# RWKV projections by way of DRAM, one eviction per scan half step and a pinned TensorE order in a hybrid decoder layer

## The chip, the cores and the metric

The kernel runs on one core of one Trainium2 chip. The metric is the device time of one execution in microseconds (us), and of several runs the median. Engines are named as the profile names them: PE (TensorE matmul), PEld (TensorE weight load, overlapping PE), DVE (VectorE), ACT (ScalarE), POOL (GpSimd), SP (SyncE, which issues most DMAs).

## What is computed

One decoder layer in fp32 for 512 prompt tokens and 8 decode tokens (520 columns, kept as two halves of 260), model width 2048:

```python
mod = silu(c) @ w_ada + b_ada                      # 6 x 2048: shift, scale, gate, twice
h = modulate(rmsnorm(x), sh1, sc1)
q, k, v, p_rwkv = split(h @ w_in)                  # 1024 + 2 x 256 attention, 3360 RWKV columns
att = banded_attention(q, k, v)                    # window 128, ALiBi, sinks
# RWKV-7, 16 heads of 64: per token, with decay w, a = -kk, b = kk * iclr
S = S * w + (S a) b^T + v k^T ;  y = S r           # then group norm, bonus, gate
x = x + gt1 * (concat(att, rw) @ w_out)
x = x + gt2 * (swiglu(modulate(rmsnorm(x), sh2, sc2)))
y = rmsnorm(x)
```

New key and value rows, the RWKV states and the last projection rows are outputs too.

## The kernel before, in words

**Main products.** All large products are built from `mm3` (L94): a weight tile is split into a high part `wh` (ACT cast, L88) and a low part `wl` (DVE, L91), and three fp32r products (`wh` by the high and low part of the activations, `wl` by the high part), each for two halves of 260 columns, make six main products per 128 rows of contraction. `main_tile` (L103) does one 128-column tile of `w_in`: 16 times six products into a PSUM tile `pm`, with a 256 KB weight load (`raw`, SP) per 24 products. After every six it calls `pump`.

**Background jobs.** Everything else in the RWKV phase consists of Python generators on the list `bg`. `pump` (L123) is a turn: it moves a model clock on and lets each job whose modelled time has come issue its next piece, up to the next `yield`. The model clock is kept by `Paced` (L30): each operation that a job issues through `self.px` adds an estimated duration to its engine's clock. That fixes the program order; the tile scheduler then reorders the instructions of each engine by a model of its own, so that the order of TensorE is the scheduler's. Line L49, in `Paced`, is the line that the profile shows for everything issued through it.

**The jobs.** `ada_gen` (L304) computes the four later parts of `mod`: for each of 16 x 16 steps a 256 KB load `ar` (a ring of three buffers in the pool `w`) and four products with 32 columns side by side (`ada`, L314), and two yields. For each of the eight head pairs `hp`: `rwkv_prep1` (L547) makes decay, key and removal factors from the key columns; `rwkv_prep2` (L641) does receptance, value and bonus; `rwkv_rest` (L690) solves a triangular system per chunk of 32 tokens on DVE (`Tt`, 31 steps, its input `As` by way of DRAM), runs the scan, and then group norm and gate.

**The scan.** For each of 16 chunks (L742 on) there are two half steps, each in a turn of its own. First, for each of the two heads `e`, a product of `L3` with the state `Z[:, c, e]` into 32 rows of the PSUM tile `psc`, at array columns 96 and 64; DVE evicts head 0 and ACT head 1 into `Z`. Second, for each head a product with `LS` into 64 rows, at array columns 0 and 64; DVE and ACT evict them, multiplied by the chunk decay `PC`, as the next chunk's state. The profile's names are `psc<-Z,L` for the first half step and `psc<-Z,LS` for the second (a digit at a name's end is left out, so `L3` reads `L`).

**Where the projections wait.** The RWKV tiles of `w_in` (8 + hp key, hp receptance, 16 + hp value) are evicted by ACT straight into one of four SBUF buffers `pc` (`w_in_tile`, L440). The main stream therefore waits for a free buffer; while it would wait it takes `filler` tiles (L452): the 12 attention tiles, which ACT copies to a buffer `sp` of the `ar` ring and SP stores to DRAM (L463).

Of the kernel before, what the change touches and what calls it, by code (L numbers as in the profile page):

```python
# [28 lines left out]
I_WA, I_G0, I_G1 = 24, 25, 26  # L29

# [21 lines left out]

class PacedCore:
# [10 lines left out]
class Kern:  # L64
    def __init__(self, tc, I, O, upto="all"):
        self.tc, self.nc, self.I, self.O, self.upto = tc, tc.nc, I, O, upto
# [67 lines left out]
    def start(self, gen):  # L134
        self.bg.append([gen, 0.0])
# [13 lines left out]
    def run(self):  # L149
        tc, nc, I = self.tc, self.nc, self.I  # L150
        R = dict(side="right")
        with ExitStack() as st:
# [3 lines left out]
            self.load_consts()  # L156
            self.catd = [self.dr.tile([P, 512], F32, name=f"catd{i}") for i in range(16)]
# [10 lines left out]
            with ExitStack() as st2:  # L168
# [28 lines left out]
                self.drain()  # L197
                right.close()
# [105 lines left out]
    def ada_gen(self):  # L304
        nc = self.px
        for c in (GT1, SH2, SC2, GT2):
            for q in range(4):
                ci = c // 4 + q
                ps = self.hold("ada")
                for k in range(KD):  # L310
# [8 lines left out]
                    yield  # L319
                    yield  # L320
# [49 lines left out]
    def startup(self):  # L370
# [25 lines left out]
        self.pcs, self.ring, self.used = {}, [], set()  # L396
# [5 lines left out]
        self.start(self.seq(self.h_parts(xk, rstd), self.ada_gen()))  # L402
# [72 lines left out]
    def rwkv_phase(self):  # L475
# [36 lines left out]
        nc.scalar.copy(self.SG1[64:128], self.SG1[0:64].bitcast(F32))  # L512
        pairs = [{"ready": True, "done": True, "chain": True, "prep1": True, "solved": True}] * 3
        for hp in range(8):
            d = {"hp": hp, "prev": pairs[-1], "prev2": pairs[-2], "prev3": pairs[-3]}
            pairs.append(d)
            for idx, job in ((8 + hp, self.seq(self.rwkv_prep1(d), self.rwkv_rest(d))), (hp, None),
                             (16 + hp, self.rwkv_prep2(d))):
                if idx not in self.pcs:
                    self.w_in_tile(idx)  # L520
                if job:
                    self.start(job)
# [14 lines left out]
    def recip(self, t, n=4):  # L537
        w = 512 // n
        for i in range(n):
            self.px.vector.reciprocal(t[:, i * w:(i + 1) * w], t[:, i * w:(i + 1) * w])  # L540
            yield

# [4 lines left out]
    def rwkv_prep1(self, d):  # L547
        nc, I, rp, rc = self.px, self.I, self.rp, self.rc
        hp = d["hp"]
        while not {"ready", "prep1"} <= d["prev"].keys() or "done" not in d["prev3"]:  # L550
            yield
# [7 lines left out]
        d["PC"] = PC = rc.tile([P, 16], F32, tag="PC", bufs=3, name=self.nm("PC"))  # L559
# [4 lines left out]
        for _ in range(3):  # L564
            yield
# [7 lines left out]
        nc.scalar.activation(A, pw, AF.Tanh, bias=self.w0h[:, hp:hp + 1], scale=0.5)  # L573
        ta = t512("tD")
# [19 lines left out]
        yield from self.recip(nrm)  # L594
# [8 lines left out]
        yield  # L603
# [4 lines left out]
        nc.vector.tensor_copy(PC, c3(B)[:, :, 31])  # L608
        d.update(kf=kf, B=B, KB=KB, t512=t512)
        yield  # L610
# [7 lines left out]
        while "solved" not in d["prev"]:  # L618
            yield
# [15 lines left out]
        q2[0].dma_start(self.ABd[hp].rearrange("(q c) t s -> (c t) q s", c=4), AB)  # L635
        for g in range(4):
            q2[g % 2].dma_start(self.As[32 * g:32 * g + 32].rearrange("p (t s) -> p t s", s=32), self.ABd[hp])
        d["prep1"] = True
        yield

    def rwkv_prep2(self, d):  # L641
        nc, I, rp, rc = self.px, self.I, self.rp, self.rc
        while "kf" not in d or "done" not in d["prev2"]:
            yield
# [1096 lines left out]
```

## Time and profile before

| | |
|---|---|
| median of 3 runs | 2659.92 us (2652.76 to 2669.23) |
| profiled execution | 2657.76 us, span 2656.0 us, mean granted TensorE clock 0.985 |
| start and first norm | 0 to 137 us |
| RWKV phase, from the first `ada` product to the first output projection | 137 to 927 us |
| attention and output projection | 927 to 1209 us |
| FFN in | 1209 to 2130 us |
| FFN out | 2130 to 2656 us |

The page gives busy times per engine; the windows give them by stage. A matmul's end is modelled and matmuls overlap, so a PE busy share near one says little: what the spacing of products is, is read from the starts in the timeline. In the groups, "idle" is an engine's idle time just before such instructions, with what ended it. A row of a tile's view gives shortest, median and longest duration in ns.

### The profile page before, as it was taken

The numbers are of one execution on the slowest core, as the hardware profiler recorded it, in microseconds if no ns is written. First come the engines' busy times: TensorE is split into PE (matmuls) and PEld (weight loads), VectorE is DVE, ScalarE is ACT, GpSimd is POOL, SyncE is SP. The second block draws the span as 40 slices with busy tenths as digits, with TensorE's granted clock in tenths as the row PEclk, the third lists the DMA queues.
The fourth block names the chain that finished last, engine by engine and source line by source line (L and its number), as shares of the span: only waits on it lengthen the run. The fifth ranks groups of instructions, "written<-read, shape, count | busy, mean of one in ns | idle before, by whom it ended". The sixth has DMA issues, their size and how long they took to land. (4 is left out here: it accounts for less than half of the span.)

```text
span 2656.0 us, 59166 instructions
## 1 busy us (share of the span) xinstructions
PE 2554.5 (96%) x23373; PEld 2340.7 (88%) x23373; DVE 1723.8 (65%) x3880; ACT 1105.9 (42%) x2153; POOL 382.5 (14%) x525
## 2 busy tenths in 40 slices
PE   7899999999999999998999999999999999999997
PEld 4677777888787889898999999999999999999997
DVE  5466767777657444678777777777777763444456
ACT  3133444545533324547544444444444532222225
POOL 0012112112112000021111212111121100000004
PEclk9999999999989999999999999999999999999999
DMA  9855445455546675245777777777777552333333
GB/s 347 294 165 154 152 126 162 149 166 160 159 153 207 203 251 146 94 160 183 191 201 204 193 208 198 191 207 198 194 208 200 155 184 92 124 125 102 116 105 106
DMA packets 241704, 460.22 MB, mean 173 GB/s; under 512 B 32353, under 2 KB 44561, under 8 KB 241393
## 3 DMA queue, kind: packets, MB, share of 16 engines
q1 hardware_dynamic: 206880, 379.88, 44.5%
q0 software_dynamic: 33904, 75.50, 13.4%
q8 instruction: 183, 3.00, 0.5%
q10 hardware_dynamic: 640, 1.05, 0.2%
q14 instruction: 97, 0.79, 0.1%
HBM read 421.73 MB, written 35.59 MB: 172 GB/s over the span
## 5 line engine op out<-in xcount | busy, mean ns | idle before, releaser
L88 ACT CAST wh<-raw 128x512 fp32r<-128x512 f32 (+2 forms) x410 | 246.9, 606 | 510.5 <-PE pf L98 278.9
L98 PE MATMUL pf<-go,wh 128*128 128x260 f32 x2560 | 414.1, 281 | 0.0
L91 DVE TENSOR_TENSOR wl<-raw,wh 128x512 fp32r<-128x512 f32 (+2 forms) x410 | 283.8, 694 | 200.4 <-ACT wh L88 194.8
L98 PEld LDWEIGHTS pf<-go,wh 128*128 128x128 f32 x2560 | 354.0, 188 | 0.1
L98 PE MATMUL pm<-hH,wh 128*128 128x260 f32 (+1 forms) x1248 | 301.3, 319 | 7.3 <-ACT wh L88 6.7
L1269 ACT CAST wh<-sr 128x512 fp32r<-128x512 f32 x320 | 198.1, 621 | 261.7 <-PE pm L1439 232.0
L1270 DVE TENSOR_TENSOR wl<-sr,wh 128x512 fp32r<-128x512 f32 x320 | 220.6, 690 | 83.0 <-ACT wh L1269 75.9
L98 PE MATMUL pm<-hH,wl 128*128 128x260 f32 (+1 forms) x1248 | 265.4, 292 | 5.2 <-DVE wl L91 5.1
L98 PE MATMUL pf<-go,wl 128*128 128x260 f32 x1280 | 267.7, 282 | 0.0
L1439 PE MATMUL pm<-xT,wh 128*128 128x260 f32 x1408 | 263.2, 286 | 4.4 <-DVE pc L1516 4.3
L98 PE MATMUL pm<-hL,wh 128*128 128x260 f32 (+1 forms) x1248 | 263.4, 291 | 0.0
L1439 PE MATMUL pm<-T,wh 128*128 128x260 f32 x1408 | 257.6, 283 | 0.0
L98 PEld LDWEIGHTS pm<-hH,wh 128*128 128x128 f32 (+1 forms) x1248 | 196.5, 191 | 57.8 <-issue 31.6
L1439 PEld LDWEIGHTS pm<-xT,wh 128*128 128x128 f32 x1408 | 216.9, 188 | 11.0 <-DVE pc L1516 6.1
L1439 PEld LDWEIGHTS pm<-T,wh 128*128 128x128 f32 x1408 | 216.9, 188 | 0.0
L98 PEld LDWEIGHTS pm<-hH,wl 128*128 128x128 f32 (+1 forms) x1248 | 197.4, 192 | 16.0 <-DVE wl L91 8.7
L1439 PE MATMUL pm<-B0H,wl 128*128 128x260 f32 x704 | 201.4, 286 | 9.6 <-DVE wl L1270 9.1
L98 PEld LDWEIGHTS pm<-hL,wh 128*128 128x128 f32 (+1 forms) x1248 | 196.9, 191 | 7.5 <-issue 5.2
L1439 PE MATMUL pm<-B0H,wh 128*128 128x260 f32 x704 | 200.3, 285 | 2.0 <-DVE acct L1206 1.7
L98 PEld LDWEIGHTS pf<-go,wl 128*128 128x128 f32 x1280 | 200.9, 188 | 0.0
L1439 PE MATMUL pm<-B0L,wh 128*128 128x260 f32 x704 | 198.9, 282 | 0.0
L1439 PE MATMUL pm<-T,wl 128*128 128x260 f32 x704 | 198.7, 282 | 0.0
(427 smaller groups left out, 5243.8 us busy)
## 6 DMA issues: line engine op xcount, KB each, us to landing
ar<-in_w_ada SPq DMA_DIRECT2D x256, 256.0 KB, 3.1
sr<-in_w_fi SPq DMA_DIRECT2D x176, 256.0 KB, 4.6
raw<-in_w_fo SPq DMA_DIRECT2D x176, 256.0 KB, 2.6
raw<-in_w_in SPq DMA_DIRECT2D x144, 256.0 KB, 3.7
araw<-in_w_ada SPq DMA_DIRECT2D x64, 512.0 KB, 6.5
raw<-in_w_fi SPq DMA_DIRECT2D x120, 256.0 KB, 4.6
s<-in_w_fi SPq DMA_DIRECT2D x80, 256.0 KB, 4.4
s<-in_w_fi POOLq DMA_DIRECT2D x80, 256.0 KB, 5.1
```

Of the source, the lines that this page charges most:

```text
L88: nc.scalar.copy(wh[:, :n], raw[:, :n])
L91: nc.vector.tensor_tensor(wl[:, :n], raw[:, :n], wh[:, :n].bitcast(F32), ALU.subtract)
L98: nc.tensor.matmul(ps[:m, bank, :HB], w, a[:, k, h, :], start=first and i == 0, stop=last and i == 2, skip_group_check=True,)
L1269: nc.scalar.copy(H, src)
L1270: nc.vector.tensor_tensor(L, src, H.bitcast(F32), ALU.subtract)
L1439: nc.tensor.matmul(ps[:, :HB], x[:, s], y, start=g == k == i == 0, stop=g == 1 and k == 3 and i == 2, skip_group_check=True)
```

## The change

- A tile of `w_in` now always goes from PSUM by ACT to a buffer `sp` of the `ar` ring and by SP to DRAM (`pwd`); a new job `fetch_pc` reads it back into a `pc` buffer, in the order in which the pairs need them, when the tile is made and the buffer four places back is used. The main stream waits for no `pc` buffer and takes no filler in between; all jobs are started at once, ahead of the 22 tiles.
- `pump` issues jobs only at every second call in this phase (`every` = 2: every twelfth main product); a job may be up to 0.5 us of model time early, and `ada_gen` comes last in a turn. `ada_gen` yields three times in four steps instead of eight times.
- TensorE's instructions are pinned to program order in this phase (`InOrder`). The new call stands at L64, so the profile of the changed kernel shows most of TensorE's instructions under that line.
- The scan: both heads' products of a half step stand at the same array columns (96; then 0), side by side in PSUM's free dimension. ACT evicts both after the first, DVE both after the second, with a `PC` of both heads in one tile (one small DMA per pair, on ACT's queue).
- In the preparation several yields are removed, so that more is issued in one turn; two waits for DMA round trips get a due time 4 us later; the `lora` buffer is guarded by `take_lf`; the wait for `solved` moves behind the store of `AB`.

The core of the diff:

```diff
     def pump(self, us=0.62):
 
         self.now(us)
-        for job in list(self.bg):
-            if job[1] > self.now():
+        self.calls += 1
+        if self.calls % self.every:
+            return
+        for job in sorted(self.bg, key=lambda job: job[2]):
+            if job[1] > self.now() + SLACK * (self.every - 1):
                 continue
...
     def w_in_tile(self, idx):
+
         nc = self.nc
-        src, m = self.w_in_src(idx)
-        while len(self.ring) >= 4 and self.ring[-4] not in self.used and len(self.spills) > 2:
-            self.filler()
-        ps = self.main_tile(src, self.hH, self.hL, m)
-        while len(self.ring) >= 4 and self.ring[-4] not in self.used:
-            self.pump()
-        pc = self.new_pc(idx)
-        nc.scalar.copy(pc[:m, 1:513].rearrange("p (h t) -> p h t", h=2), ps[:m, :, 0:256])
-        nc.scalar.copy(self.SC[:m, idx], ps[:m, :, 255:260])
+        ps = self.main_tile(self.I["w_in"][idx], self.hH, self.hL)
+        t = self.w.tile([P, 512], F32, tag="ar", bufs=3, name=self.nm("sp"))
+        nc.scalar.copy(t.rearrange("p (h t) -> p h t", h=2), ps[:, :, 0:256])
+        nc.scalar.copy(self.SC[:, idx], ps[:, :, 255:260])
+        nc.sync.dma_start(self.pwd[idx], t)
+        self.made.add(idx)
+
+    def fetch_pc(self, order):
+        for idx in order:
+            while idx not in self.made or self.ring[-4:][0] not in self.used and len(self.ring) >= 4:
+                yield
+            pc = self.new_pc(idx)
+            del self.pcs[idx]
+            self.nc.sync.dma_start(pc[:, 1:513], self.pwd[idx])
+            self.done_at = self.now() + 3.5
+            yield
+            self.pcs[idx] = pc
+            yield
...
         for c in range(16):
             ps = self.aux_c(hp % 2)
-            for e, o in ((0, 96), (1, 64)):
-                nc.tensor.matmul(ps[o:o + 32, 0:64], L3[:, e, c // 4, (c % 4) * 32:(c % 4) * 32 + 32], Z[:, c, e],
-                                 start=True, stop=True, skip_group_check=True, tile_position=(0, o))
-            nc.vector.tensor_copy(Z[96:128, c, 0], ps[96:128, 0:64])
-            nc.scalar.copy(Z[96:128, c, 1], ps[64:96, 0:64])
-            self.done_at += 0.2
-            yield
-            dst = Z[0:64, c + 1] if c < 15 else SF
             for e in range(2):
-                ro = slice(64 * e, 64 * e + 64)
-                nc.tensor.matmul(ps[ro, 64:128], LS[:, e, c, :], Z[:, c, e], start=True, stop=True, skip_group_check=True,
-                                 tile_position=(0, 64 * e))
+                nc.tensor.matmul(ps[96:128, 64 * e:64 * e + 64], L3[:, e, c // 4, (c % 4) * 32:(c % 4) * 32 + 32], Z[:, c, e],
+                                 start=True, stop=True, skip_group_check=True, tile_position=(0, 96))
+            nc.scalar.copy(Z[96:128, c], ps[96:128, 0:128].rearrange("p (e i) -> p e i", e=2))
+            yield
             for e in range(2):
-                ro = slice(64 * e, 64 * e + 64)
-                if e:
-                    nc.scalar.activation(dst[:, e], ps[ro, 64:128], AF.Copy, scale=PC[ro, c:c + 1])
-                else:
-                    nc.vector.tensor_scalar(dst[:, e], ps[ro, 64:128], PC[ro, c:c + 1], None, ALU.mult)
-            self.done_at += 0.2
+                nc.tensor.matmul(ps[0:64, 128 + 64 * e:192 + 64 * e], LS[:, e, c, :], Z[:, c, e], start=True, stop=True,
+                                 skip_group_check=True, tile_position=(0, 0))
+            nc.vector.tensor_tensor(
+                Z[0:64, c + 1] if c < 15 else SF, ps[0:64, 128:256].rearrange("p (e i) -> p e i", e=2),
+                PC[0:64, :, c:c + 1].broadcast_to([64, 2, 64]), ALU.mult)
             yield
```

How the instructions move is seen best in the order. TensorE in the middle of a scan, before (`pm` main products, `ada` the modulation products, `psc` the scan):

```order
L49 MATMUL psc<-Z_1732,L_283_1776 32x64 x2
L98 MATMUL pm_3647<-hH,wh_3706 128x260 x2
L98 MATMUL pm_3647<-hL,wh_3706 128x260 x2
L98 MATMUL pm_3647<-hH,wl_3707 128x260 x2
L49 MATMUL adT_3737<-cst,adar_3722 128x128
L49 MATMUL psc<-Z_1732,LS_1736 64x64 x2
L98 MATMUL pm_3647<-hH,wh_3706 128x260
L314 MATMUL ada_3740<-ar_3741,cT 32x128 x4
L98 MATMUL pm_3647<-hH,wh_3706 128x260
L98 MATMUL pm_3647<-hL,wh_3706 128x260 x2
L98 MATMUL pm_3647<-hH,wl_3707 128x260 x2
```

The same engine after, in the middle of two scans:

```order
L64 MATMUL psc<-Z_1756,L_283_1800 32x64 x2
L64 MATMUL psc<-Z_1757,L_377_2411 32x64 x2
L64 MATMUL ada_3981<-ar_4048,cT 32x128 x4
L64 MATMUL pm_3950<-hH,wh_4026 128x260 x2
L64 MATMUL pm_3950<-hL,wh_4026 128x260 x2
L64 MATMUL pm_3950<-hH,wl_4027 128x260 x2
L64 MATMUL pm_3950<-hH,wh_4026 128x260 x2
L64 MATMUL pm_3950<-hL,wh_4026 128x260 x2
L64 MATMUL pm_3950<-hH,wl_4027 128x260 x2
L64 MATMUL psc<-Z_1756,LS_1760 64x64 x2
L64 MATMUL psc<-Z_1757,LS_1762 64x64 x2
L64 MATMUL ada_3981<-ar_4078,cT 32x128 x4
```

Groups of small products, scattered before among six or fewer mains, now stand together between runs of twelve mains; two pairs' scans (`Z_1756`, `Z_1757`) share turns. From the first `ada` product to the first output projection the order lists 410 such groups before and 238 after, with the same products.

SP around a tile's end, before, one of the attention tiles (`qd` is its place in DRAM):

```order
L49 DMA ar_10173<-in_w_ada 128x512
L463 DMA qd_100<-sp_10145 128x512
L49 DMA ar_10205<-in_w_ada 128x512
L86 DMA raw_10525<-in_w_in 128x512
L49 DMA ar_10254<-in_w_ada 128x512
```

And after, an RWKV tile (`pwd` is its place in DRAM, `pc` the buffer it is read back into):

```order
L50 DMA ar_4307<-in_w_ada 128x512
L479 DMA pwd_91<-sp_4234 128x512
L50 DMA ar_4338<-in_w_ada 128x512
L110 DMA raw_4626<-in_w_in 128x512
L50 DMA ar_4344<-in_w_ada 128x512
L488 DMA pc_4251<-pwd_91 128x512
L50 DMA ar_4406<-in_w_ada 128x512
```

A store, and for 22 tiles a read back behind it, stand between the loads for `ada` on the same queue. Before the last `ar` load there are 10 such stores before the change and 24 after.

More of the change, by code (lines that the diff above doesn't have):

```diff
@@ L132, in pump, with start @@
             job[1] = self.done_at
[L134 to L135 removed]
+    def start(self, gen, late=False):
+        self.bg.append([gen, 0.0, late])
     def drain(self):
@@ L156, in run @@
             self.load_consts()
+            self.pwd = [self.dr.tile([P, 512], F32, name=f"pwd{i}") for i in range(24)]
             self.catd = [self.dr.tile([P, 512], F32, name=f"catd{i}") for i in range(16)]
@@ L512, in rwkv_phase @@
         nc.scalar.copy(self.SG1[64:128], self.SG1[0:64].bitcast(F32))
+        self.pinned, self.every = True, 2
         pairs = [{"ready": True, "done": True, "chain": True, "prep1": True, "solved": True}] * 3
+        order = [i + hp for hp in range(8) for i in (8, 0, 16)]
+        order = [i for i in order if i not in self.pcs]
+        self.start(self.fetch_pc(order))
         for hp in range(8):
@@ L516, in rwkv_phase @@
             pairs.append(d)
[L517 to L522, printed above, removed]
+            self.start(self.seq(self.rwkv_prep1(d), self.rwkv_rest(d)))
+            self.start(self.rwkv_prep2(d))
+        for idx in order:
+            self.w_in_tile(idx)
         return pairs[-1]
@@ L563, in rwkv_prep1 @@
         nc.scalar.activation(sq, k, AF.Square, scale=col(P_KK))
-        for _ in range(3):
-            yield
+        self.done_at = max(self.done_at, self.now() + 3)
+        yield
         pw = self.aux("pw")
@@ L781, in rwkv_rest @@
         d["chain"] = True
+        yield from self.take_lf()
+        wh, wl = self.lora(hp, 384)
+        nc.scalar.copy(wh[64:128, 128:256], wl[64:128, 128:256].bitcast(F32))
         yield
```

74 lines of the change are left out of this document (50 added, 24 removed).

## The prediction

> **What bounds the kernel now.** I read the page's busy table first, then the windows by stage, then the waits on single tiles, then the timeline of one engine at a few places.
>
> ```profile
> PE 2554.5 (96%) x23373; PEld 2340.7 (88%) x23373; DVE 1723.8 (65%) x3880; ACT 1105.9 (42%) x2153; POOL 382.5 (14%) x525
> ```
>
> ```profile
> 137.00:927.00 790.00, 759.30 (x8462) 618.25 (x8456) 530.18 (x1371) 339.91 (x730) 141.64 (x196) 0.97 0.53 164
> 1209.00:2130.00 921.00, 906.29 (x7397) 892.98 (x7398) 693.55 (x1204) 441.92 (x752) 170.23 (x220) 1.00 0.74 196
> ```
>
> The second fence holds two windows: length, then busy time of PE, PEld, DVE, ACT, POOL, then granted clock, DMA share, GB/s. TensorE bounds both stages, but not in the same way. In the FFN (second window) a main product of 128x260 comes every 921.00/7397 = 0.12 us. In the RWKV phase (137 to 927 us, first `ada` product to first output projection) PE looks 96% busy too, yet its weight loader is busy 78% of the time against 97%. The order lists 3372 main products there; at 0.12 us they need 405 us of the 790. The other 385 us are small fp32 products, what it costs to switch to them and back, and waits. (The granted clock is 0.97 there against 1.00: up to 24 us that steadier work might give back; it stands in no sum.) The change touches this phase alone: on every engine the order after it is the same. So all that follows is about those 385 us.
>
> **What one interruption costs.** Four pieces of the PE timeline (start, length, line, operands, count):
>
> ```profile
> 148.01 0.39 PE L98 MATMUL pm<-hH,wl 128*128 128x260 f32 x2
> 148.33 0.42 PE L314 MATMUL ada<-ar,cT 128*32 128x128 f32 x8
> 148.68 0.51 PE L98 MATMUL pm<-hH,wh 128*128 128x260 f32 x2
> 149.03 0.41 PE L98 MATMUL pm<-hL,wh 128*128 128x260 f32 x2
> ```
>
> ```profile
> 328.25 0.40 PE L98 MATMUL pm<-hH,wl 128*128 128x260 f32 x2
> 328.58 0.31 PE L49 MATMUL psc<-Z,L 128*32 128x64 f32 x4
> 328.82 0.51 PE L98 MATMUL pm<-hH,wh 128*128 128x260 f32 x2
> 329.16 0.28 PE L98 MATMUL pm<-hL,wh 128*128 128x260 f32 x1
> ```
>
> ```profile
> 266.80 0.40 PE L98 MATMUL pm<-hH,wl 128*128 128x260 f32 x2
> 267.13 0.43 PE L314 MATMUL ada<-ar,cT 128*32 128x128 f32 x8
> 267.39 0.28 PE L49 MATMUL psc<-Z,L 128*32 128x64 f32 x4
> 267.60 0.51 PE L98 MATMUL pm<-hH,wh 128*128 128x260 f32 x2
> 267.94 0.40 PE L98 MATMUL pm<-hL,wh 128*128 128x260 f32 x2
> ```
>
> From the last main pair before the group to the second pair after it, two pairs (0.48 us) would pass without a group. What is over is the group's price: `ada` alone 149.03 - 148.01 - 0.48 = 0.54 us; the first half of a scan step alone 329.16 - 328.25 - 0.48 = 0.43; both together 267.94 - 266.80 - 0.48 = 0.66. One interruption fewer thus saves 0.54 + 0.43 - 0.66 = 0.31 us. The second half of a step uses a 128x64 array, and going from the 32-wide `ada` to it costs again:
>
> ```profile
> 297.07 0.39 PE L98 MATMUL pm<-hH,wl 128*128 128x260 f32 x2
> 297.40 0.43 PE L314 MATMUL ada<-ar,cT 128*32 128x128 f32 x8
> 297.75 0.34 PE L49 MATMUL psc<-Z,LS 128*64 128x64 f32 x4
> 298.02 0.50 PE L98 MATMUL pm<-hH,wh 128*128 128x260 f32 x2
> 298.36 0.40 PE L98 MATMUL pm<-hL,wh 128*128 128x260 f32 x2
> ```
>
> ```profile
> 391.87 0.40 PE L98 MATMUL pm<-hL,wh 128*128 128x260 f32 x2
> 392.10 0.28 PE L98 MATMUL pm<-hH,wl 128*128 128x260 f32 x1
> 392.31 0.34 PE L49 MATMUL psc<-Z,LS 128*64 128x64 f32 x4
> 392.57 0.39 PE L98 MATMUL pm<-hH,wl 128*128 128x260 f32 x1
> 392.80 0.41 PE L98 MATMUL pm<-hH,wh 128*128 128x260 f32 x2
> ```
>
> Together 298.36 - 297.07 - 0.48 = 0.81; alone 392.80 - 391.87 less four mains (0.48) = 0.45; a merge of these saves 0.54 + 0.45 - 0.81 = 0.18.
>
> **The change, part by part.**
>
> 1. *Fewer turns, fixed order.* The order shows the same instructions on TensorE (1024 `ada`, 512 scan products, 3372 mains, and so on), in 238 interruptions of the main stream instead of 410. 172 fewer, at 0.18 to 0.31 us: -31 to -53 us. The merged groups are of both sorts, so I take the middle, 0.245: **-42 us**.
>
> 2. *Both heads of a step on the same array columns.* The two products of a half step sat on separate array columns (96 and 64; 0 and 64) and ran side by side; now both stand at 96, and both at 0, one behind the other. Side by side they added 0.66 - 0.54 = 0.12 us to an `ada` interruption; one behind the other they need that twice. 256 half steps x 0.12 = **+31 us**. Bounds: 0 if the second hides behind `ada`'s four products, +50 if the whole of 0.81 - 0.54 = 0.27 comes twice for the 128 second halves.
>
> 3. *One eviction per half step.* These rows are of the scan's PSUM tile: two of its evictions (shortest/median/longest ns), then what the instructions on it waited for, in us, and how often.
>
> ```profile
> L49 ACT COPY Z<-psc x128: 203/203/206, 271.1 to 884.5; 32x64 f32<-32x64 f32 x128
> L49 DVE TENSOR_SCALAR Z<-psc,PC x120: 265/276/278, 272.9 to 882.8; 64x64 f32<-64x64 f32 x120
> ```
>
> ```profile
>   DVE Z L49: 197.2, 160
>   PE psc L49: 104.7, 113
>   ACT Z L49: 40.6, 72
> ```
>
> ACT's eviction of the second head waited 197.2 us for DVE's of the first; TensorE then waited 40.6 us in 72 places for ACT. The chain was PE, DVE, ACT, PE; it becomes PE, ACT, PE and PE, DVE, PE. I estimate the copies of 128 columns at 0.26 us on ACT and 0.34 on DVE, between the rows above (64 columns) and those below (512), by length. Busy time that this saves on DVE and ACT lies off the path and counts nothing; the work that hides it is the main products. What counts is the 40.6 us. After the change at least twelve mains (1.45 us) and mostly an `ada` (0.54) lie between a half step and its successor, 2.0 us; the chain needs about 0.3 (product) + 0.34 + one queued 128x512 operation:
>
> ```profile
> L91 DVE TENSOR_TENSOR wl<-raw,wh 128x512 fp32r<-128x512 f32 (+2 forms) x146 | 105.3, 723 | 52.4 <-ACT wh L88 48.8 <-PE pY L49 2.0 <-PE pm L98 0.4
> ...
> L49 DVE TENSOR_TENSOR stmp<-Tt,As 128x60 f32<-128x60 f32 (+24 forms) x248 | 69.6, 281 | 16.1 <-DMA As<-ABd 9.9
> ...
> L49 ACT COPY Z<-pV 32x512 f32<-32x512 f32 x32 | 18.5, 577 | 6.8 <-PE pV L49 6.3
> ```
>
> 0.3 + 0.34 + 0.72 = 1.4 us, so it is late only where two long operations stand ahead. I leave 8 us: **-32 us**. Bounds -40 and, if TensorE held to its order waits where the scheduler had slipped mains in between, +10.
>
> The Trainium skill, TensorEngine Tiling (Array Packing), under PSUM Bottleneck, advises to evacuate PSUM with both ScalarE and VectorE. That speaks against this edit; here the two evictions ran one behind the other (the 197.2 us), so the trace does not bear it out for this step.
>
> 4. *Inputs through DRAM.* 22 product tiles now leave through an `ar` buffer and SyncE (22 stores, 22 reads back). The `ar` ring has three buffers and is `ada`'s prefetch; the order puts 24 such stores before the last `ada` load, where there were 10. The waits of `ada` for its load before 713 us (one store) and from 713 to 911 us (nine stores), SyncE's own waits for stores, and the landing time of an `ar` load (the last number):
>
> ```profile
>   DMA ar<-in_w_ada: 13.8, 9
> ```
>
> ```profile
>   DMA ar<-in_w_ada: 10.0, 15
> ```
>
> ```profile
> SPq L463 <- ACT sp L461: 23.2, 7, 10.2
> ```
>
> ```profile
> ar<-in_w_ada SPq DMA_DIRECT2D x253, 256.0 KB, 3.1
> ```
>
> The nine stores cost 10.0 us, 1.1 us each; 24 cost 26, so **+16 us**. Queued behind a waiting store or read on SyncE are the next `ada` and weight loads; the weights have three buffers of 24 mains each and stay covered, `ada` has about two turns against a landing of 3.1 us. Bounds: 0, and a full landing each, 24 x 3.1 - 10 = +64. The store's copy replaces one of the same size on ACT: nothing.
>
> 5. *Later due times and joined turns in the preparation.* DVE waited 9.9 us for `As` (the row above); that may go. Against it, the transpose of `at` now stands in the same turn as its DVE operations: eight times up to two of 0.72 us. I take 0, bounds -10 and +12.
>
> Sum: -42 + 31 - 32 + 16 = -27 us. The profiled execution took 2657.76 us (span 2656.0), 2 us under the median of 2659.92. **2657.8 - 27 = 2631 us.**
>
> **Rivals.** (a) *The scan's waits stay*: in a fixed order each late eviction stops TensorE, so the 40.6 us remain. For it: TensorE waited 40.6 us although the scheduler had chosen the order. Against: the pairs of 12 mains. Time 2657.8 - 42 + 31 + 16 = 2663, no change. (b) *The eviction by one engine is slower*, the skill's rule as a mechanism of this kernel: each half step takes 0.34 - 0.28 = 0.06 us longer, 256 x 0.06 = 15 us on top of (a): 2678, by rows still within 1%. (c) *The `ar` ring starves*, the slower side: store, read back and two `ada` in one turn share three buffers and one queue, and TensorE can no longer run mains ahead of a late `ada`. It turns the sum positive from (27 + 26)/24 = 2.2 us per store on; at a landing of 3.1 us and the scan's waits kept, 2663 - 16 + 64 = 2711. For it: SyncE stood 23.2 us behind seven stores, up to 10.2 us. Against: 1.1 us each so far. (d) *The second head costs nothing and no wait is left*: 2657.8 - 42 - 40 - 10 = 2566 at the outside; with half of parts 2 and 4 as well, 2589.
>
> **How the numbers follow.** About 1%, 27 us, is what a measurement can tell from no change here. The forecast gets 0.50, its own range 2612 to 2650; as 2633 is the 1% line and it lies near, 0.34 of this counts as faster, 0.16 as no change. (a) gets 0.20 and (b) 0.04, nearly all no change (0.21) with 0.03 slower; (c) 0.13: 0.10 slower, 0.03 no change; (d) 0.13, faster. Faster 0.47, same 0.40, slower 0.13. The range leaves out the outer half of (c) and (d): 2588 to 2682.
>
> **What would show each step.** Part 1: fewer, longer groups between runs of twelve mains, at 0.5 us or more. Part 2: the four records of a half step spread over 0.4 us instead of 0.3. Part 3: no ACT wait for DVE's `Z`, and TensorE's waits on `Z` under 10 us. Part 4: `ada` waiting some 30 us for `ar`, after tile ends. The prediction is wrong if the phase's length changes by the waits alone and not by the groups, if `ada`'s waits pass 50 us, or if anything after the first output projection moves.

## The result and the profile after

The changed kernel takes 2775.38 us (median of 4 runs, 2774.89 to 2778.0) against 2663.77 for the kernel before in the same runs: 1.0418 times, interval 1.038 to 1.0456. The forecast was 2631 us, the range ended at 2682. The sign is wrong, and the time lies 93 us outside.

Busy times of TensorE and its weight loader, from the page after:

```profile
PE 2589.7 (93%) x23373; PEld 2381.1 (86%) x23373; DVE 1680.5 (61%) x3752; ACT 1064.5 (38%) x2019; POOL 376.6 (14%) x525
```

Two windows after, the RWKV phase and the FFN (length, busy of PE, PEld, DVE, ACT, POOL, granted clock, DMA share, GB/s):

```profile
138.40:1045.50 907.10, 788.41 (x8461) 652.78 (x8461) 488.00 (x1243) 298.76 (x595) 136.16 (x196) 0.94 0.50 155
1331.30:2250.30 919.00, 905.31 (x7398) 893.83 (x7399) 692.70 (x1202) 441.50 (x752) 170.28 (x219) 1.00 0.74 197
```

The FFN takes what it took (919 us against 921). The RWKV phase grew from 790 to 907 us, with the same products: PE is busy 87% of it, where it was 96%. So nearly all of the loss lies in the phase that the change touches: 88 of the 117 us are time in which PE stands idle (119 us against 31), and 29 us are longer busy time. TensorE's own waits in that phase, the longest rows before (total us, times, longest):

```profile
PE psc L49 <- ACT Z L49: 14.0, 22, 1.6
PE ada L314 <- DMA ar<-in_w_ada: 11.0, 12, 2.9
```

And after:

```profile
PE ada L64 <- DMA ar<-in_w_ada: 55.8, 37, 4.3
PE psc L64 <- DVE Z L50: 19.6, 27, 3.9
PE psc L64 <- ACT Z L50: 15.6, 31, 2.1
PE pu L64 <- DVE TT L50: 5.4, 1, 5.4
...
PE psc L64 <- DVE L L50: 3.0, 7, 0.4
```

`ada` waits for its loads 45 us longer, the scan (the three `psc` rows) for its evictions 24 us longer; all rows of that view together are 118.0 us after and 29.2 before. Here is what the two kinds look like. First, a turn in which the scans of two pairs meet (timeline after: start, length, engine, line, operation; in brackets the idle time before, and what ended it):

```profile
621.89 0.41 PE L64 MATMUL psc<-Z,L 128*32 128x64 f32 x4
622.34 0.26 ACT L50 COPY Z<-psc 32x128 f32<-32x128 f32 x1 [0.67 <-PE psc L64]
622.65 0.24 PE L64 MATMUL psc<-Z,L 128*32 128x64 f32 x1 [0.35 <-ACT Z L50]
622.66 0.32 PE L64 MATMUL ada<-ar,cT 128*32 128x128 f32 x3
```

Both pairs' products write `psc`, one PSUM tile of one bank, each in columns of its own. The second pair's product, next in the pinned order, starts only when ACT has copied the first pair's result out: 0.57 us after that pair's last product began at 622.08, where products of one group follow each other by 0.06. In second half steps the same gap is 0.66 us, with DVE's eviction in it. Of the scan's 38 us of waits 34 stand where its product directly follows another scan product. The Trainium skill, PSUM — Partial Sum Buffer (PSUM bank collisions raise a hardware error), asks to keep engines apart by bank and quadrant of 32 partitions, not by address; both pairs' first half steps use the same 32 partitions, and the trace agrees that the product waits although its columns are others. Whether the bank or the shared tile is what holds the product back is not shown: no run gave the two pairs tiles in two banks.

Second, a late load at a tile's end (the rows of SyncE's queue, SPq, with the TensorE groups around them):

```profile
508.19 0.42 PE L64 MATMUL ada<-ar,cT 128*32 128x128 f32 x8
...
509.79 0.33 SPq L110 DMA_DIRECT2D raw<-in_w_in  x1
...
509.98 0.58 ACT L477 COPY sp<-pm 128x512 f32<-128x512 f32 x1
510.17 0.45 PE L64 MATMUL psc<-Z,LS 128*64 128x64 f32 x4
...
510.59 0.33 SPq L479 DMA_DIRECT2D pwd<-sp  x1
...
511.02 1.11 SPq L50 DMA_DIRECT2D ar<-in_w_ada  x2
...
514.51 0.65 PE L64 MATMUL ada<-ar,cT 128*32 128x128 f32 x8 [3.90 <-DMA ar<-in_w_ada]
515.10 0.58 PE L64 MATMUL pm<-hH,wh 128*128 128x260 f32 x1
```

The `ada` group of this turn was due behind the scan, at about 510.6. Its load left SyncE at 511.02, behind the store of the tile, and TensorE stood 3.90 us with twelve main products ready behind it in the order. Three windows around the place, in the columns of the windows above:

```profile
505.00:511.00 6.00, 5.62 (x56) 4.37 (x54) 4.65 (x9) 1.80 (x5) 0.10 (x1) 1.00 0.13 44
511.00:514.30 3.30, 0.00 (x0) 0.00 (x0) 1.44 (x3) 0.00 (x0) 0.00 (x0) 1.00 0.85 280
514.30:517.70 3.40, 3.19 (x20) 2.80 (x20) 0.43 (x1) 0.41 (x1) 0.00 (x0) 0.51 0.77 243
```

After the wait of 3.90 us the granted clock is 0.51 for the next 3.4 us: such a wait is paid a second time. In the whole phase TensorE stood at half clock for 112.6 us after and 41.0 before (the stretches at 0.5 in the clock's records), 36 us of work at the most. The Trainium skill, TensorE: Matmul & The Clock Gate (HAM oscillation), gives about 3.4 us without products as what brings the half clock back; the trace agrees at this place. Most stretches at half clock came behind shorter waits, though (last section).

### The profile page after: what moved, and what is told of

It is laid out like the page before. It is cut to its first block, busy times and chain, and to the rows that moved or that the text cites. A ratio compares the mean times of both kernels' runs of the same rounds, so it can differ in the third digit from the quotient of the medians.

```text
span 2776.2 us, 58978 instructions
## 1 busy us (share of the span) xinstructions
PE 2589.7 (93%) x23373; PEld 2381.1 (86%) x23373; DVE 1680.5 (61%) x3752; ACT 1064.5 (38%) x2019; POOL 376.6 (14%) x525
## 5 line engine op out<-in xcount | busy, mean ns | idle before, releaser
L64 PE MATMUL pf<-go,wh 128*128 128x260 f32 x2560 | 414.1, 282 | 0.0
L64 PEld LDWEIGHTS pf<-go,wh 128*128 128x128 f32 x2560 | 354.2, 188 | 0.1
L64 PE MATMUL pm<-hH,wh 128*128 128x260 f32 (+1 forms) x1248 | 290.7, 315 | 6.2 <-ACT wh L112 5.5
L64 PE MATMUL pm<-hH,wl 128*128 128x260 f32 (+1 forms) x1248 | 263.8, 294 | 6.8 <-DVE wl L115 6.7
L64 PE MATMUL pm<-xT,wh 128*128 128x260 f32 x1408 | 263.5, 286 | 6.5 <-DVE pc L1562 6.5
L64 PE MATMUL pf<-go,wl 128*128 128x260 f32 x1280 | 267.8, 283 | 0.0
L64 PE MATMUL pm<-hL,wh 128*128 128x260 f32 (+1 forms) x1248 | 262.0, 293 | 0.0
L64 PE MATMUL pm<-T,wh 128*128 128x260 f32 x1408 | 257.6, 283 | 0.0
L64 PEld LDWEIGHTS pm<-hH,wh 128*128 128x128 f32 (+1 forms) x1248 | 198.5, 196 | 64.5 <-issue 51.4
L64 PEld LDWEIGHTS pm<-xT,wh 128*128 128x128 f32 x1408 | 217.2, 189 | 13.0 <-DVE pc L1562 8.2
L64 PEld LDWEIGHTS pm<-T,wh 128*128 128x128 f32 x1408 | 217.0, 188 | 0.0
L64 PEld LDWEIGHTS pm<-hH,wl 128*128 128x128 f32 (+1 forms) x1248 | 201.8, 197 | 13.7 <-DVE wl L115 10.0
L64 PE MATMUL pm<-B0H,wl 128*128 128x260 f32 x704 | 200.5, 285 | 6.6 <-DVE wl L1316 6.2
L64 PEld LDWEIGHTS pm<-hL,wh 128*128 128x128 f32 (+1 forms) x1248 | 201.8, 197 | 3.2 <-issue 2.9
L64 PE MATMUL pm<-B0H,wh 128*128 128x260 f32 x704 | 200.2, 284 | 2.2 <-DVE acct L1252 1.7
L64 PEld LDWEIGHTS pf<-go,wl 128*128 128x128 f32 x1280 | 201.2, 188 | 0.0
L64 PE MATMUL pm<-B0L,wh 128*128 128x260 f32 x704 | 199.0, 283 | 0.0
L64 PE MATMUL pm<-T,wl 128*128 128x260 f32 x704 | 198.8, 282 | 0.0
```

The lines of the kernel that those rows point to most:

```text
L64: ins = f(*a, **kw)
```

## The experiments

Eighteen kernels ran, in five groups, each beside runs of the kernel before on the same chip. "Over before" is the median less the median of the kernel before in the same group, "waits" the sum of TensorE's wait rows in the RWKV phase, "half clock" the time at clock 0.5 there, "groups" the number of interruptions of the main stream in the records (one fewer than by the order).

| kernel | over before, us | ratio (interval) | waits (ada, scan) | half clock | groups |
|---|---|---|---|---|---|
| before | 0 | 1 | 29.2 (11.0, 14.0) | 41.0 | 409 |
| changed | +111.6 | 1.0418 (1.038 to 1.0456) | 118.0 (55.8, 38.2) | 112.6 | 237 |
| e1 stores on ACT's queue | +110.8 | 1.0416 (1.0389 to 1.0442) | 114.9 (46.0, 42.7) | 119.5 | 237 |
| e2 evictions at the turn's end | +75.0 | 1.0277 (1.0246 to 1.0307) | 92.0 (55.3, 6.0) | 95.6 | 238 |
| e3 not pinned | +20.4 | 1.0073 (1.0054 to 1.0092) | 18.7 (6.7, 0.7) | 41.0 | 402 |
| e4 pinned, turns at every sixth | +130.0 | 1.0482 (1.046 to 1.0504) | 112.6 (31.2, 13.2) | 109.2 | 426 |
| e5 not pinned, old scan | +16.1 | 1.0066 (1.0041 to 1.009) | 27.8 (12.5, 5.9) | 34.1 | 411 |
| e6 before, new scan | +17.7 | 1.0069 (1.0038 to 1.0101) | 22.9 (13.5, 3.2) | 34.1 | 419 |
| e7 before, pinned | +44.1 | 1.0164 (1.0126 to 1.0203) | 80.2 (23.5, 24.3) | 64.9 | 339 |
| e8 no ada loads | +54.1 | 1.0213 (1.0173 to 1.0253) | | | |
| e9 ada free, evictions late | +63.6 | 1.0251 (1.0221 to 1.0282) | 81.7 (54.8, 4.9) | 112.6 | 252 |
| e10 e9 with old columns | +60.5 | 1.0235 (1.0212 to 1.0258) | 97.1 (51.2, 23.0) | 75.1 | 268 |
| e11 own store buffer | +60.4 | 1.0235 (1.0216 to 1.0253) | 85.6 (17.1, 37.1) | 75.1 | 237 |
| e12 e5 with turns at every sixth | +56.4 | 1.021 (1.0184 to 1.0236) | 41.2 (12.3, 6.4) | 95.6 | 474 |
| e13 own buffer, evictions late | +38.1 | 1.0127 (1.0093 to 1.0162) | 64.8 (19.4, 5.2) | 68.3 | 238 |
| e14 e5 with own buffer | -6.2 | 0.9966 (0.9946 to 0.9986) | 27.4 (3.4, 7.6) | 34.1 | 352 |
| e15 before, turns at every twelfth | +55.7 | 1.0201 (1.0174 to 1.0228) | 89.3 (4.9, 49.2) | 125.9 | 312 |
| e16 e5 with ada first in a turn | +16.1 | 1.0051 (1.0028 to 1.0074) | 34.0 (11.7, 10.7) | 30.7 | 412 |
| e17 three pc buffers | +112.4 | 1.0423 (1.0394 to 1.0453) | 120.0 (56.5, 38.7) | 92.2 | 237 |
| e18 e13 with old columns | +55.1 | 1.0202 (1.0176 to 1.0229) | 94.8 (20.8, 36.9) | 85.3 | 238 |

In e8 attention moved into the phase, so that its stage numbers are not comparable.

**Is it SyncE's queue, or the ring? (e1, e11, e17, e8)** In e1 the stores (the attention tiles' too) leave from ACT's queue and the reads back from POOL's:

```diff
-        nc.sync.dma_start(self.pwd[idx], t)
+        nc.scalar.dma_start(self.pwd[idx], t)
-            self.nc.sync.dma_start(pc[:, 1:513], self.pwd[idx])
+            self.nc.gpsimd.dma_start(pc[:, 1:513], self.pwd[idx])
```

> The changed kernel, with the stores of projection tiles issued on ACT's queue (the engine that has just copied the tile) and the reads back on POOL's, so that SyncE holds only loads for ada and weights (and the small ones that it had). Theory 1 (the ada loads stand on SyncE behind a store that waits for its copy): TensorE's waits of ada for its load fall from 55.8 us to under 20, and with fewer half-clock stretches the time falls by 35 to 55 us, to 2720 to 2740. Rival (the buffers are what lacks: the store's tile sits in the three-buffer ring): the ring is as before, the waits stay above 40 us, the time within 15 us of 2775. Rival (pinning and pairs of ada are at fault): no change either.

No change: theory 1, the queue, fell. SyncE no longer holds a store, but a row has come up there that shows the ring:

```profile
SPq L50 <- DMA pwd<-sp: 29.1, 15, 4.9
```

A load on that line waits until a store has landed, 15 times; of the loads there, those of `ar` share their buffers with the store's tile. So e11 gave the 22 RWKV stores a buffer of their own, in the room of one of four `pc` buffers, and left them on SyncE:

```diff
-        t = self.w.tile([P, 512], F32, tag="ar", bufs=3, name=self.nm("sp"))
+        t = self.rp.tile([P, 520], F32, tag="spo", bufs=1, name=self.nm("sp"))[:, 0:512]
```

> The changed kernel, pinned, with the RWKV tiles' stores in a buffer of their own instead of the three-buffer ring of ada's loads (room for it comes from a ring of three instead of four pc buffers). Theory of the shared ring: ada's waits fall from 55.8 to under 35 us and the time by 20 us or more, under 2755. Rival (the loads are late by their place on SyncE's queue and by the pinned order, whatever the ring): waits above 45 us, time within 12 us of 2775.

51 us came back (111.6 to 60.4), and `ada`'s waits went from 55.8 to 17.1:

```profile
PE psc L64 <- ACT Z L50: 17.2, 31, 2.1
PE ada L64 <- DMA ar<-in_w_ada: 17.1, 13, 3.0
PE psc L64 <- DVE Z L50: 16.9, 27, 2.8
```

The end of the same tile in e11, SyncE's and TensorE's rows:

```profile
476.15 5.73 SPq L50 DMA_DIRECT2D ar<-in_w_ada  x4
...
480.68 0.43 PE L64 MATMUL ada<-ar,cT 128*32 128x128 f32 x8
...
482.46 0.59 ACT L477 COPY sp<-pm 128x512 f32<-128x512 f32 x1
...
482.66 0.44 PE L64 MATMUL psc<-Z,LS 128*64 128x64 f32 x4
...
483.03 0.43 PE L64 MATMUL ada<-ar,cT 128*32 128x128 f32 x8
483.08 0.33 SPq L479 DMA_DIRECT2D pwd<-sp  x1
```

Four loads have left in the 7 us ahead of the store, where it was one in the changed kernel, and `ada` starts at 483.03, right behind the scan and without a wait. Over all 22 stores, 42.5 of `ada`'s 55.8 us of waits end in the 8 us behind a store in the changed kernel, and 3.2 of 17.1 in e11. So the rows read that with the ring shared one of three buffers goes to the store, and the loads that come after it in the ring can only be put late. e17 is the control for the smaller `pc` ring that e11 needed:

```diff
-        pc = pool.tile([P, 520], F32, tag=tag, bufs=4 if tag == "pc" else 1, name=self.nm("pc"))
+        pc = pool.tile([P, 520], F32, tag=tag, bufs=3 if tag == "pc" else 1, name=self.nm("pc"))
```

> The changed kernel with a ring of three pc buffers instead of four, and nothing else: the control for the two runs with a store buffer of their own. If it was the store's place in ada's ring that cost: no change or a little slower, 2770 to 2790, waits of ada still about 55 us. If fewer reads ahead were what helped: 2725 to 2755.

It did nothing (+112.4), so in the pinned order the 51 us are the store's place in the ring. e8 prices all late loads at once, by leaving the loads out:

```diff
-                    nc.sync.dma_start(raw, self.I["w_ada2"][ci - 8, k])
...
-                            ps[32 * j:32 * j + 32, 0:128], self.cT[:, k, :], raw[:, j * 128:(j + 1) * 128],
+                            ps[32 * j:32 * j + 32, 0:128], self.cT[:, k, :], self.ident,
```

> The changed kernel (pinned) with the 256 loads for ada left out: the products read a constant instead, so mod is not computed. It prices the late loads whole. Theory: the 55.8 us of waits go, and half-clock stretches with them (112.6 us of half clock in the phase to about 60, 10 to 25 us): 65 to 90 us, to 2685 to 2710. Rival (another wait takes their place, on the scan or the preparation, since turns then come sooner): the gain stays under 40 us, over 2735.

57.5 us came back: less than the theory's 65, well over the rival's 40. The late loads may cost more than that, for without them the main products end ahead of the scans, and in the last 55 us of the phase TensorE stood idle for 26. The ring's 51 us are most of it.

**Two scans in one PSUM tile (e2).** The evictions of a half step are collected, and issued when every job has had its turn (the due time of a half step is set 0.7 us later in their place):

```diff
+        for f in self.post:
+            f()
...
-            nc.scalar.copy(Z[96:128, c], ps[96:128, 0:128].rearrange("p (e i) -> p e i", e=2))
+            self.post.append(lambda: nc.scalar.copy(Z[96:128, c], ps[96:128, 0:128].rearrange("p (e i) -> p e i", e=2)))
```

> The changed kernel, with the two evictions of a scan half step issued at the end of the turn, behind the products of every job in that turn. Theory 2 (where two pairs' scans meet in one turn, the second pair's product waits for the first pair's eviction, since both lie in one PSUM bank): the 0.57 and 0.66 us gaps between the two pairs' products go, TensorE's waits of psc on Z fall from 35 us to under 15, and the time falls by 15 to 30 us. Rival (the waits come from the scan's own chain, now pinned): the gaps stay or move to the next turn, no change within 8 us.

36.6 us came back, somewhat over the expectation; the scan's waits fell to two rows of 3.0, `ada`'s stayed:

```profile
PE ada L64 <- DMA ar<-in_w_ada: 55.3, 36, 5.5
...
PE psc L64 <- ACT Z L50: 3.0, 3, 2.4
PE psc L64 <- DVE Z L50: 3.0, 5, 1.0
```

**Pinning and turns (e3, e4, e7).** The first line below is e3 and the second e4; the third, with the class `InOrder`, is all that e7 adds to the kernel before.

```diff
-        self.pinned, self.every = True, 2
+        self.pinned, self.every = False, 2
...
+        self.pinned, self.every = True, 1
...
+        self.pinned = True
```

> The changed kernel, with TensorE's order left to the scheduler again in the RWKV phase (turns still at every twelfth product). Rival theory (in a pinned order each late load or eviction stops TensorE, where the scheduler had put main products in between): the sum of TensorE's waits falls from some 115 us to under 60 and the time by 50 us or more. Theory 1 and 2 (a queue behind stores, one bank): the scheduler can hide a part only; the time falls by 0 to 40 us, and the waits of ada for its load stay above 35 us.

91 us came back with one word. The rival theory held; the other one, by which late loads stay above 35 us, was wrong: they fell to 6.7 in all.

```profile
PE ada L64 <- DMA ar<-in_w_ada: 6.7, 10, 1.2
PE pu L64 <- DVE TT L50: 3.3, 1, 3.3
```

With the order free, the scan waits 0.7 us in all and `ada` hardly for its loads; the merging is undone too, with 402 groups where the pinned order has 237.

> The changed kernel, pinned, with turns at every sixth main product as before the change. Theory (fewer turns save some 25 to 40 us of switches, but bring two loads' need at once): switches come back, about +30 us, and the ada waits fall by some 20 us: time 2765 to 2795. Rival (turns in pairs are what starves the loads and makes two scans meet): the waits fall by over 60 us and the time goes down by 30 us or more.

Turns at every sixth product are 18 us slower at nearly the same sum of waits, for 189 groups more: about 0.1 us for each. The edit also takes back the slack and `ada_gen`'s fewer yields, so that this is a price of all three. `ada`'s waits fell by 25 us as expected, but those of `pu`, the products with the solved system, rose to 31 us in their place. The rival, that joined turns are the whole loss, fell.

> The kernel before with TensorE pinned to program order in the RWKV phase, and nothing else. Theory (a product that reads a late load or eviction stops everything behind it once the order is fixed): waits of TensorE rise from 29 us to over 80, time +50 us or more, over 2715. Rival (pinning hurts only with joined turns and two loads per turn): waits under 50 us, time within 20 us of 2665.

44 us, just under the theory's 50 with its waits just over 80: pinning by itself, without joined turns or more stores, costs half of what it costs in the changed kernel.

**The scan by itself (e5, e6).** e6 puts the new scan (and its `PC` of both heads) into the kernel before, e5 the old one into the unpinned kernel:

```diff
-            for e, o in ((0, 96), (1, 64)):
-                nc.tensor.matmul(ps[o:o + 32, 0:64], L3[:, e, c // 4, (c % 4) * 32:(c % 4) * 32 + 32], Z[:, c, e],
...
+            for e in range(2):
+                nc.tensor.matmul(ps[96:128, 64 * e:64 * e + 64], L3[:, e, c // 4, (c % 4) * 32:(c % 4) * 32 + 32], Z[:, c, e],
```

> The kernel before with the scan step of the change alone (both heads on the same columns, one eviction per half step). By the forecast: +31 for the serial products less 32 for the chain's waits, no change within 8 us. By what the traces show now (TensorE's own waits for the scan were 14.0 us, not 40.6, and the products take some 30 us longer): +15 to +30 us, 2680 to 2695.

+17.7, as the traces said and not as the forecast did.

> The changed kernel, TensorE not pinned, and the scan step as before the change (heads on separate array columns, an eviction by each of two engines). What is left of the change are DRAM passes, turns and due times. Theory (serial products cost 27 to 36 us, the other parts nothing): 27 us under the unpinned kernel's 2687, so 2655 to 2665, no difference from before. Rival (the DRAM passes cost what is left, the scan nothing): within 8 us of 2687.

The expectation was missed. By the medians over before the old scan gives back 4 us, by the phases of the two profiled executions 15 (819.5 to 804.0); e5's runs spread from 2670 to 2698. Either way some 16 us over before remained that were not the scan.

**What is left (e12, e14, e15, e16).** e12 takes the unpinned kernel with the old scan back to turns at every sixth product (and so, as in e4, to the old yields and no slack), e16 puts `ada` first in its turns, e14 gives it e11's store buffer, and e15 puts `every` = 2, the 0.5 us of slack and `ada_gen`'s fewer yields into the kernel before:

```diff
-        self.pinned, self.every = True, 2
+        self.pinned, self.every = False, 1
...
-        for job in sorted(self.bg, key=lambda job: job[2]):
+        for job in sorted(self.bg, key=lambda job: not job[2]):
```

> The unpinned kernel with the old scan (2678, before 2662) with turns at every sixth main product again. What is left of the change are the DRAM passes and the regrouped preparation. If the turns cost the 16 us that were left: 2655 to 2668. If the DRAM passes or the regrouping cost them: 2672 to 2685.

Far outside both expectations, at +56.4. With the regrouped preparation, turns at every sixth product leave 474 groups and 95.6 us of half clock; here the rarer turns are worth 40 us.

> The unpinned kernel with the old scan, ada first in a turn instead of last. Ahead of the scan's first half step ada leaves the array at the same width (0.66 us for both in the kernel before, against 0.77). If the place in the turn costs a good part of the 16 us: 2663 to 2672. If not: within 5 us of 2678.

Nothing: the place of `ada` in the turn is not it.

> The unpinned kernel with the old scan (2678) and the stores in a buffer of their own. If the shared ring costs the 16 us that are left to the kernel before: 2660 to 2668. If not (ada's waits were 12.5 us there): within 5 us of 2678.

22 us came back, more than hoped: the shared ring costs the unpinned kernel as well, although `ada`'s recorded waits there were only 12.5 us. At 0.9966 (0.9946 to 0.9986) of the time before this is the one version that is faster than both kernels, by a third of a per cent; single runs overlap (2642 to 2666 us against 2653 to 2672). The control for three `pc` buffers, e17, was run in the pinned order alone.

> The kernel before with turns at every twelfth main product, 0.5 us of slack and ada's fewer yields, and nothing else. By the forecast's first term, unpinned (the scheduler scatters the groups again, 402 of them in the unpinned kernel): no gain, within 8 us of 2663; if jobs issued at half the pace make the chain of a pair late: +10 to +40. If turns in pairs are worth what the kernel with the old scan showed (42 us): 2620 to 2640.

Turns at every twelfth product in the kernel before cost 56 us, more than any guess. The jobs come at half the pace with all their old yields, and the scan becomes the chain that TensorE waits for. The last main product starts at 842 us, with 143 us of the phase still to come, 119 of them at half clock. 37 half steps there follow directly on another, most of them 1.06 to 1.28 us apart:

```profile
PE psc L49 <- ACT Z L49: 48.4, 58, 2.9
PE pYx L49 <- DVE ys L49: 11.6, 1, 11.6
```

**Can the pinned order be mended? (e9, e10, e13, e18)** e9 is e2 with `ada`'s products outside the pinning, e10 that with the old columns and evictions (issued late too), e13 is e2 and e11 together, e18 that with the old columns.

```diff
-                        self.nc.tensor.matmul(
+                        self.nc.tensor.eng.matmul(
                             ps[32 * j:32 * j + 32, 0:128], self.cT[:, k, :], raw[:, j * 128:(j + 1) * 128],
```

> The changed kernel with both: evictions of the scan at the end of the turn, and ada's products left out of the pinning (the scheduler places them; everything else on TensorE stays pinned). Theory (pinning costs by exactly two things, late ada loads, 60 us, and two scans in one bank, 33 us): the waits of ada fall under 15 us and those of the scan under 10; from 2742 the time falls by 55 less what lone ada groups cost again (up to 20), to 2680 to 2705. Rival (other pinned jobs become late instead): total waits stay above 70 us, time above 2715.

The rival's numbers came (81.7 us of waits, 2727 us) without its mechanism: not other jobs became late, but `ada`, freed from the pinning, still waits 54.8 us. Why the scheduler left them behind late loads is not shown.

> As the kernel with free ada and late evictions, but with the scan's products on separate array columns and two evictions, as before the change. By the two runs on the scan alone (+17.7 us in the kernel before, -9.4 us back in the unpinned one) 9 to 18 us less than the kernel with the new scan: 2662 to 2695. It is the version that should come nearest to the kernel before, and may beat it if pinned turns keep their groups together (under 2650).

The expectation of 9 to 18 us less was missed: only 3 us under e9. The products take less, but the scan's waits are back at 23.0.

> The changed kernel, pinned, with both causes mended: the RWKV tiles' stores in a buffer of their own and the scan's evictions at the end of a turn. If they add up: 2775 - 51 - 33 = 2691, within 10; waits of TensorE under 55 us, half clock under 60 us. If they share their gain (a scan that waits less makes ada come sooner, and later loads): 2705 to 2720. If pinned groups then pay at last: under 2675.

By differences 73.5 us come back, where the two single runs sum to 51.2 + 36.6 = 87.8: they add up for the greater part, and the time is just within the 10 us of the first expectation. The waits are not: 64.8 us remain instead of under 55, on late loads (19.4), `pt` (18.9, transposes) and `pu` (6.3).

> The changed kernel, pinned, with stores in a buffer of their own, evictions of the scan at the end of a turn, and the old scan's separate array columns with two evictions. The serial products cost 17 us net: 2700 - 17 = 2683, within 10, and the rest to the unpinned kernel's 2655 (some 28 us) is what pinning costs beyond those three. If pinning costs nothing more: 2650 to 2662. If the two evictions in one bank make the pinned products wait again (23 us in the kernel with free ada): no gain, 2695 to 2710.

The last expectation held in kind and the loss was larger: with the old scan the pinned kernel is 17 us slower (55.1 against 38.1), though its products take less. The waits on the tile `psc`, in e18 and then in e13:

```profile
  PEld psc L64: 48.9, 54
  PE psc L64: 36.9, 36
```

```profile
  PEld psc L64: 7.9, 11
  PE psc L64: 5.3, 7
```

In e18 all of these TensorE waits stand behind a run of main products and none behind a neighbour's scan: with two evictions behind each other the chain is too long for the pinned twelve products; with one it mostly fits. The new scan is right for the pinned order, and wrong for the scheduler's.

## Why the prediction was wrong, point by point

The step that failed is the pricing of the waits. The forecast took waits that the scheduler's order had left over as the price of the same evictions and loads in a fixed order, and gave the pinning no term; measured, the pinning cost 91 us in the changed kernel (e3), for the greater part through `ada`'s late loads and through scans that share a PSUM tile.

**Part 1, fewer interruptions, -42.** The merging took place (237 groups), but in the pinned order turns at every second call instead of every call were worth 18 us for 189 groups (e4, with slack and yields in it), 0.10 us each against 0.18 to 0.31. The prices of single merged groups had been read rightly; that such a group meets a bank or a load that is not ready was not in them.

**Part 2, serial products, +31.** Right. Two interruptions by one half step alone, after:

```profile
955.07 0.40 PE L64 MATMUL pm<-hH,wl 128*128 128x260 f32 x2
955.39 0.41 PE L64 MATMUL psc<-Z,L 128*32 128x64 f32 x4
955.74 0.51 PE L64 MATMUL pm<-hH,wh 128*128 128x260 f32 x2
956.09 0.40 PE L64 MATMUL pm<-hL,wh 128*128 128x260 f32 x2
```

```profile
922.72 0.40 PE L64 MATMUL pm<-hH,wl 128*128 128x260 f32 x2
923.06 0.45 PE L64 MATMUL psc<-Z,LS 128*64 128x64 f32 x4
923.43 0.51 PE L64 MATMUL pm<-hH,wh 128*128 128x260 f32 x2
923.78 0.41 PE L64 MATMUL pm<-hL,wh 128*128 128x260 f32 x2
```

956.09 - 955.07 - 0.48 = 0.54 us, where it was 0.43; 923.78 - 922.72 - 0.48 = 0.58, where it was 0.45. 128 x (0.11 + 0.13) = 31 us. That these two places stand for the rest is borne out by the other lone half steps at full clock: their medians went from 0.44 to 0.54 us (first) and from 0.46 to 0.57 us (second), which gives 27 us.

**Part 3, "I leave 8 us: -32 us".** This step failed twice. Its 40.6 us were too large: the tile's view before has under them

```profile
  PEld psc L49: 26.8, 51
  PE psc L49: 14.0, 22
```

the weight loader's waits and TensorE's, which lie over one another in time; only 14.0 could be won, so that the scan edit alone came out at +17.7 (e6). And "at least twelve mains (1.45 us) and mostly an `ada` (0.54) lie between a half step and its successor" looked at one pair: the order shown with the change has two pairs' products behind each other, and the second waits for the first's eviction. The scan's waits became 38.2 us instead of 8; 36.6 us came back when the evictions stood behind both products (e2). The mechanism itself, that one eviction shortens the chain, was right where the order is pinned (e18 against e13).

**Part 4, "24 cost 26, so +16 us".** The place was right and the size was not: `ada`'s waits rose by 45 us, and the shared ring's part of the time was 51 us (e11). The estimate per store came from an order in which the scheduler could put main products ahead of late loads; there the ring cost 22 us (e14), not far from the 16. The 10.0 us under it again count the weight loader and TensorE side by side: TensorE's own part was 4.2 us, so that a right reading would have given less still. Rival (c) had the mechanism in half: the ring starves and TensorE cannot run mains ahead of a late `ada`; its 13 in 100 were too low, and its 2711 lay 64 us under the measured time; the 37 us of the shared PSUM tile, for which it had no term, are one part of that, and the rest was not assigned. The read back and the queue were in that rival too: moving both off SyncE did nothing (e1).

**Part 5, 0.** Not seen apart; with ring and scan as they should be, and no pinning, all that is left of the change is worth 6 us (e14).

**The pinning itself** had no term. It stood in a bound of part 3 (+10) and in rivals (a) and (c). Measured, it was 91 us in the changed kernel (e3) and 44 in the kernel before (e7). From before to after, in one order of steps: -6.2 for turns, due times and DRAM (e14), +22.3 for the ring (e5 less e14), +4.3 for the scan (e3 less e5; +17.7 by e6), +91.2 for the pinning. Of these 91 us the ring and the shared PSUM tile, mended together, give back some 51 (73.5 of e13 less the 22.3). What remains of the pinned kernel's loss when both are mended (38 us, e13) was not settled further.

Of the marks named ahead, "`ada`'s waits pass 50 us" came true, "the phase's length changes by the waits alone and not by the groups" came true in the main (88 of 117 us), and nothing after the first output projection moved.

## What to carry to other kernels

An order that the scheduler has chosen hides late loads and evictions; the waits that its trace shows are what could not be hidden, and no estimate for the same kernel in a fixed order. Before fixing an order, ask of each joined group which PSUM tile it shares with its neighbour and which load it reads, and give buffers that are taken early and freed late (a store's) a ring of their own. Add waits by one engine's rows only: a tile's view counts the weight loader and TensorE side by side.

## What the runs showed of the hardware

A wait of 3.90 us cost up to 1.7 us again, at a granted clock of 0.51 for the next 3.4 us; 20 stretches at half clock lay in the phase after, 7 before. Only 5 of the 20 have a wait of 3.4 us or more in the 6.8 us ahead of them; ahead of the other 15 the longest was 1.8 to 3.3 us. And an eviction of both heads takes little longer than one of one head: 258 ns on ACT for the first half step (before 203, and 230 on DVE), 282 ns on DVE for the second (before 276, and 311 on ACT):

```profile
L50 ACT COPY Z<-psc x128: 257/258/262, 272.4 to 995.5; 32x128 f32<-32x128 f32 x128
L50 DVE TENSOR_TENSOR Z<-psc,PC x120: 220/282/284, 277.9 to 993.2; 64x128 f32<-64x128 f32 x120
```

The prediction had estimated 0.26 and 0.34 us, by length.
